# Differential attention: head outputs normalized once per head with tokens on partitions, and the second softmax map scaled by two factors in one GpSimd operation

## The chip, the cores and the metric

The kernel runs on one core of a Trainium2 chip. The time is the device time of one execution in microseconds (us). Five engines matter: TensorE (PE, matmuls), VectorE (DVE), ScalarE (ACT), GpSimd (POOL) and SyncE (SP, which here only issues DMAs). Each engine works through its own instructions in order and waits on semaphores of the others. DMAs of one issuing queue are requested in order.

## The reference, cut to what matters

A trunk of two layers on a sequence of 1024 tokens with model width 1024. The change lies in the first layer's differential attention with 12 heads: each head has two softmax maps, whose difference, weighted by a learned `lam_full`, is applied to the values; the result of every token and head is then normalized over its 128 channels.

```python
def diff_attention(u, positions, lam, subln_g, lambda_init):
    ...
    lam_full = jnp.exp(jnp.sum(lf[0] * lf[1])) - jnp.exp(jnp.sum(lf[2] * lf[3])) + lambda_init
    ...
        p = jax.nn.softmax(s, axis=-1)
        w = p[:, :, 0] - lam_full * p[:, :, 1]
        return jnp.einsum('bhqk,bkhe->bqhe', w.astype(v.dtype), v)
    ...
    o = rms_norm(o, subln_g) * (1.0 - lambda_init)

def rms_norm(x, g):
    xf = x.astype(jnp.float32)
    y = xf * lax.rsqrt(jnp.mean(xf * xf, axis=-1, keepdims=True) + EPS)
    return (y * g.astype(jnp.float32)).astype(x.dtype)
```

Around it stand an input projection, a memory attention, a gate `silu(gate)` and an output projection; the second layer has multi-scale pooling in place of the attention.

## The kernel before

**Stages.** A prologue normalizes the input and builds tables (rotary angles, and `lambda_full`, L571, which leaves the pair `coef` = [1, −lam_full] on every partition). Then the attention stage runs head by head; its end leads into the memory attention, the output projection of layer 0, and layer 1.

**Precision.** Activations and weights are split into a high and a low part (`hh`/`hl`, `wh`/`wl`, `kb`/..., suffix h and l), and each product is made of three passes (`mm3`, L120 to L127). Making a low part is one subtraction on POOL or DVE (L118 for weights: `wl_q`, `wl_k`, `wl_v`, `wl_ga`).

**Order.** PE's instructions stand in the order in which the program is written (`manual_schedule` for PE). For DVE, ACT, POOL and SP a scheduler sets the order. To keep PE busy, the next head's projections (q, k, the gate `ga`, v) are cut into steps, each of three matmuls of 128x512, and `self.step(n)` puts n steps between the attention's own matmuls; there are 64 steps per head. `self.hooks` is a list of small pieces of work with due times counted in steps; `run_hooks`, called once per group of the head's loop, runs one that is due.

**One head.** `attention_layer` goes over the query blocks in pairs p = 3, 2, 1, 0, and over key pairs jj up to p. `score_block` computes the scores of one block of 128 queries (PE L851), masks and exponentiates them (`e`, DVE L856, ACT L865; the sums of the exponentials lie in `st`), and `combine` (L871) makes of the two maps one weight matrix: reciprocal of the two sums (L875), times `coef` (L876), map 1 scaled on POOL (L877), map 0 scaled and added on DVE (L880). `turn_weights` transposes the weights on PE (`wt`, L902) and splits them (`wth` L905, `wtl` L906); `apply_weights` multiplies with the values (L925) into `o`, which holds 128 channels on the partitions and 512 tokens in the row: half a head's tokens.

**Behind each half.** After p = 2 (half 1) and p = 0 (half 0) `attend_post` (L929) squares `o` on ACT (`sq`, L937), multiplies `o` by the learned gain and the gate on DVE (`og`, L938), and splits `sq` into `sqh` (ACT, L939) and `sql` (POOL, L940). It leaves a hook `norm`, due 7 steps later. `norm` multiplies a 128x128 matrix of ones by `sqh` and `sql` (PE, L947), so that every partition holds the sums of all 512 tokens; four DVE instructions (L951) take 32 partitions each and lay four stretches of 128 tokens under one another into `rsx`, 128x128, with the mean and EPS; `newton` (L234 to L241) makes the reciprocal square root in ten DVE steps; four of its rows, one per stretch, are stored to DRAM (`rs`, SP, L956), read back broadcast to all partitions (`z`, SP, L958), multiplied with `og` on POOL (L959) and stored for the output projection (`store_z`, L608).

**Beside it.** The rotary part of the next head: the projected q and k go through ACT to `rotq`/`rotk`, are multiplied by the table on POOL (L767), combined on DVE (`fk`, L764 and L768), and written as the split key `kb` (L802, L803), which the scores read. The reciprocal square root of a few columns is also made elsewhere, by `mean_square` (PE, L250: float32 matmuls with one column per 128 tokens) and `rsqrt_small` (tiles `ms_h`, `rsxh`, `rsyh`, `rsuh`). At the end of the attention stage SP loads the memory tokens (`mf`, L462), DVE splits them (L469, `ml`) and scales the memory query (`mqf`, L620), while PE runs the projections of the remaining gates (`ga`).

Of the kernel before, what the change touches and what calls it, by code (L numbers as in the profile page):

```python
# [10 lines left out]
F32 = mybir.dt.float32  # L11
F32R = mybir.dt.float32r
# [3 lines left out]
ALU = mybir.AluOpType  # L16
# [4 lines left out]
P = 128  # L21
# [3 lines left out]
HALF = 512  # L25
NH = 12
MH = 4
MEM = 256
EPS = 1e-6
# [19 lines left out]
class Trunk:  # L49
# [11 lines left out]
    def build(self):  # L61
# [6 lines left out]
        self.turns = []  # L68
        self.hh = [[None] * KT, [None] * KT]
# [218 lines left out]
    def setup(self):  # L288
        nc, tc, a, const = self.nc, self.tc, self.a, self.const
# [33 lines left out]
        self.rs_dram = [  # L323
            [self.dram.tile([4, P], F32, name=f"rs_{h}_{half}") for half in range(2)]
            for h in range(NH)
        ]
# [10 lines left out]
    def prologue(self, pool):  # L337
# [13 lines left out]
        def hidden(half, ks):  # L351
            for d in ks:
# [3 lines left out]
                    (("sq", 1), ("og", 2), ("es", 4)), alone=half == 1, by=None if half else (None, nc.vector)[d % 2],  # L356
# [214 lines left out]
    def lambda_full(self, sp):  # L571
        nc, a = self.nc, self.a
        lam = sp.tile([P, HALF], F32, tag="z", name="lam")[:, :256].rearrange(
# [3 lines left out]
        prod = sp.tile([P, HALF], F32, tag="sq", name="lam_prod")[:, :128].rearrange(  # L577
# [293 lines left out]
    def combine(self, i, es, st):  # L871
# [4 lines left out]
        nc.vector.tensor_tensor(st[:, 3, :], st[:, 3, :], self.coef, op=ALU.mult)  # L876
        nc.gpsimd.tensor_scalar(  # L877
            es[1][:, :n], es[1][:, :n], st[:, 3, 1:2], 1.0, op0=ALU.mult, op1=ALU.mult
# [50 lines left out]
    def attend_post(self, pool, h, half, o, g):  # L929
        nc = self.nc  # L930
        nm = f"{h}{half}"
        sq = pool.tile([P, HALF], F32, tag="sq", name=f"sq{nm}")
        sh = pool.tile([P, HALF], F32R, tag="sqh", name=f"sqh{nm}")
        sl = pool.tile([P, HALF], F32R, tag="sql", name=f"sql{nm}")
        og = pool.tile([P, HALF], F32, tag="og", bufs=2, name=f"og{nm}")
# [3 lines left out]
        nc.scalar.copy(sh, sq)  # L939
        nc.gpsimd.tensor_tensor(sl, sq, sh.bitcast(F32), op=ALU.subtract)  # L940

        def norm():


            t = self.tb(f"ms{nm}")
            for i, part in enumerate((sh, sl)):
                nc.tensor.matmul(t, self.ones_r, part, start=(i == 0), stop=(i == 1))  # L947
            x = pool.tile([P, P], F32, tag="rsxa", name=f"rsx{nm}")
            for j in range(4):
                p = slice(32 * j, 32 * j + 32)  # L950
                nc.vector.tensor_scalar(  # L951
                    x[p, :], t[p, j * P : (j + 1) * P], 1.0 / P, EPS, op0=ALU.mult, op1=ALU.add
                )
            y = self.newton(pool, x, P, "a")
            row = self.rs_dram[h][half]
# [752 lines left out]
```

## Time and profile before

| | before |
|---|---|
| median of three runs | 1843.32 us (1841.23 to 1845.65) |
| the profiled execution | 1850.51 us, of which the profile's span is 1848.7 us |
| mean granted clock of TensorE | 0.978 |
| DVE, work of the changed code: L876 | 96 instructions, 36.3 us busy |
| DVE: L951 | 96 instructions, median 286 ns |
| POOL: L877, L940, L959 | 76.6 us (x96), 31.9 us (x24), 31.3 us (x24) |
| ACT: L937, L939 | 14.5 us (x24), 14.9 us (x24) |

The first row is what a change is judged by; the profile is a single execution and gives the durations of single instructions. Busy times of different engines lie beside each other and don't add up to the span. In a list of instructions each row has the start, the length, the engine, the line, the operation, what is written and read (buffer numbers left out), and the shapes; in brackets the idle time of the engine before it and what ended that. A wait reads "engine, tile and line that waited <- who ended the wait: total us, times, longest us".

### The profile page before, as it was taken

Reading aid. Unit: us, or ns where it says so; the run is one execution under the profiler, and the core shown is the slowest. Engines: PE = TensorE matmul, PEld = TensorE weight load, DVE = VectorE, ACT = ScalarE, POOL = GpSimd, SP = SyncE. Lnnn points to the kernel's source line nnn. Section 1 sums busy time; section 2 is a strip of 40 time slices with the busy share of each in tenths; the row PEclk is TensorE's granted clock in tenths of the full one; section 3 lists DMA queues with packets and bytes.
Section 4 is the critical chain, followed back from the end, with each engine's and each line's share of the span. In section 5 each row is a group of like instructions: output and inputs, shape, how many; then the busy total and the mean of one; then the engine's idle time right before and its main releaser. Section 6 shows DMA issues by size and latency. Waiting matters only on the chain.

```text
span 1848.7 us, 24838 instructions
## 1 busy us (share of the span) xinstructions
PE 1744.1 (94%) x8478; PEld 1449.6 (78%) x8478; DVE 1351.3 (73%) x2705; ACT 950.3 (51%) x1764; POOL 660.3 (36%) x563
## 2 busy tenths in 40 slices
PE   6899999999999999999999998997999999979997
PEld 4788888888888888888777886875788777768886
DVE  7778789788888889876657768688876667754513
ACT  6667667657657656743246546453443332224422
POOL 4334444444434344442241243300133433413452
PEclk9999999999999999999999999998999999989998
DMA  5011111111111111112463878643312121156542
GB/s 184 23 35 54 42 44 58 46 46 47 46 46 57 36 52 52 40 64 68 152 202 121 268 255 266 224 143 108 103 61 89 55 88 66 54 173 196 171 150 95
DMA packets 81679, 188.68 MB, mean 102 GB/s; under 512 B 9200, under 2 KB 17104, under 8 KB 81552
## 3 DMA queue, kind: packets, MB, share of 16 engines
q1 hardware_dynamic: 79296, 183.08, 30.2%
q10 hardware_dynamic: 2160, 3.75, 0.6%
q8 instruction: 67, 1.10, 0.2%
q14 instruction: 60, 0.49, 0.1%
q0 software_dynamic: 96, 0.26, 0.0%
HBM read 155.29 MB, written 31.77 MB: 101 GB/s over the span
## 4 chain that ended last, share of the span: by engine, by line
PE 67%; DVE 19%; ACT 6%; DMA 5%; issue 3%; POOL 0%; SPq 0%; DVEq 0%; ACTq 0%; POOLq 0%
PE s L851 4%; PE o L925 3%; PE ob L127 3%; PE ob L125 3%; PE ob L126 3%; PE ga L125 3%; PE ga L126 3%; PE ga L127 3%; DMA zf<-z 2%; PE v L125 2%; PE v L127 2%; PE v L126 2%; PE wt L902 2%; ACT rotq L763 2%; DVE e L856 2%
## 5 line engine op out<-in xcount | busy, mean ns | idle before, releaser
L865 ACT ACTIVATE e<-e,st 128x640 f32<-128x640 f32 (+4 forms) x192 | 148.2, 773 | 111.7 <-DVE st L856 110.7
L118 POOL TENSOR_TENSOR wl_o<-wf_o,wh_o 128x384 fp32r<-128x384 f32 x64 | 98.8, 1544 | 238.4 <-ACT wh_o L115 210.9
L877 POOL TENSOR_SCALAR e<-e,st 128x640 f32<-128x640 f32 (+4 forms) x96 | 76.6, 798 | 199.1 <-DVE st L876 116.0
L1539 DVE TENSOR_TENSOR zr<-zf,zr 128x512 fp32r<-128x512 f32 x132 | 108.9, 843 | 42.8 <-ACT zr L1538 42.6
L118 DVE TENSOR_TENSOR wl_o<-wf_o,wh_o 128x640 fp32r<-128x640 f32 x64 | 59.3, 926 | 104.9 <-ACT wh_o L115 100.5
L1538 ACT CAST zr<-zf 128x512 fp32r<-128x512 f32 x132 | 80.8, 619 | 87.7 <-DMA zf<-z 60.7
L905 ACT CAST wth<-wt 128x512 fp32r<-128x512 f32 (+2 forms) x168 | 72.5, 432 | 103.4 <-PE wt L902 73.8
L115 ACT CAST wh_o<-wf_o 128x1024 fp32r<-128x1024 f32 x64 | 67.2, 1049 | 112.9 <-PE ob L126 68.4
L856 DVE CUSTOM_DVE_ANT_0 e<-s,mask 128x512 f32<-128x512 f32 (+2 forms) x192 | 109.5, 581 | 11.6 <-PE s L851 10.0
L125 PE MATMUL ga<-hh,wh_ga 128*128 128x512 f32 x256 | 105.0, 410 | 3.7 <-DVE mqf L620 3.7
L127 PE MATMUL ob<-zr,wl_o 128*128 128x512 f32 x256 | 101.0, 394 | 6.0 <-DVE wl_o L118 6.0
L127 PE MATMUL ga<-hh,wl_ga 128*128 128x512 f32 x256 | 101.6, 397 | 0.0
L126 PE MATMUL ga<-hl,wh_ga 128*128 128x512 f32 x256 | 101.5, 397 | 0.0
L851 PE MATMUL s<-kb,qa 128*128 128x512 f32 (+2 forms) x288 | 98.6, 349 | 2.9 <-DVE kb L803 2.9
L125 PE MATMUL ob<-zr,wh_o 128*128 128x512 f32 x256 | 100.8, 394 | 0.1
L126 PE MATMUL ob<-zr,wh_o 128*128 128x512 f32 x256 | 100.5, 393 | 0.0
L851 PE MATMUL s<-kb,qlo 128*128 128x512 f32 (+2 forms) x288 | 98.4, 349 | 0.0
L125 PE MATMUL k<-hh,wh_k 128*128 128x512 f32 x192 | 79.5, 414 | 8.3 <-ACT wh_k L115 8.3
L906 DVE TENSOR_TENSOR wtl<-wt,wth 128x512 fp32r<-128x512 f32 (+2 forms) x168 | 82.7, 492 | 5.8 <-ACT wth L905 4.5
L880 DVE SCALAR_TENSOR_TENSOR e<-e,st,e 128x640 f32<-128x640 f32 (+4 forms) x96 | 77.9, 811 | 9.8 <-POOL e L877 9.1
L902 PE MATMUL wt<-cst,e 128*128 128x128 f32 x432 | 69.7, 275 | 14.4 <-DVE e L880 11.9
L125 PE MATMUL q<-hh,wh_q 128*128 128x512 f32 x192 | 79.5, 414 | 0.0
(1226 smaller groups left out, 5657.0 us busy)
## 6 DMA issues: line engine op xcount, KB each, us to landing
zf<-z SPq DMA_DIRECT2D x132, 256.0 KB, 4.4
wf_o<-in_w_out SPq DMA_DIRECT2D x64, 512.0 KB, 3.9
wf_ga<-in_w_in SPq DMA_DIRECT2D x16, 512.0 KB
wf_q<-in_w_in SPq DMA_DIRECT2D x12, 512.0 KB, 3.3
wf_v<-in_w_in SPq DMA_DIRECT2D x12, 512.0 KB, 3.8
z<-rs SPq DMA_DIRECT2D x24, 256.0 KB, 3.2
z<-z SPq DMA_DIRECT2D x24, 256.0 KB, 2.0
wf_k<-in_w_in SPq DMA_DIRECT2D x11, 512.0 KB, 3.1
```

Source lines behind the costliest of these rows:

```text
L118: eng.tensor_tensor(wl[:, c], wf[:, c], wh[:, c].bitcast(F32), op=ALU.subtract)
L125: nc.tensor.matmul(out, sh, mh, start=first, stop=False, skip_group_check=more)
L126: nc.tensor.matmul(out, sh, ml, start=False, stop=False, skip_group_check=more)
L127: nc.tensor.matmul(out, sl, mh, start=False, stop=last, skip_group_check=more)
L851: nc.tensor.matmul(sc[m][:, w], q[half][part][:, m, qs], k[kh][:, m, w], start=(part == 0), stop=(part == 1),)
L856: nc.vector.tensor_tensor_reduce(out=es[m][:, lo:hi], in0=sc[m][:, : hi - lo], in1=self.mask[:, S - n + lo : S - n + hi], scale=1.0, scala ...
L865: nc.scalar.activation(es[m][:, :n], es[m][:, :n], AF.Exp, bias=least[m], scale=-1.0, accum_out=st[:, 2, m : m + 1],)
L880: nc.vector.scalar_tensor_tensor(es[0][:, :n], es[0][:, :n], st[:, 3, 0:1], es[1][:, :n], op0=ALU.mult, op1=ALU.add)
L902: nc.tensor.transpose(t[:, c : c + P], w[b][:, j * P : (j + 1) * P], self.ident)
L906: nc.vector.tensor_tensor(wl[:, lo:hi], t[:, lo:hi], wh[:, lo:hi].bitcast(F32), op=ALU.subtract)
L1538: nc.scalar.copy(z[:, 0, :], zf)
L1539: nc.vector.tensor_tensor(z[:, 1, :], zf, z[:, 0, :].bitcast(F32), op=ALU.subtract)
```

## The change

`attend_post` no longer splits the squares. For half 1 it only keeps `sq` and `og` in a list `self.posts`; behind half 0 it leaves one hook for the whole head. That hook turns the product around: the squares are the stationary side, 128 tokens at a time, and a column `inv_v` of 1/128 is the moving side, so each of 8 float32 matmuls gives the mean squares of 128 tokens, one per partition; the eight fill a tile of 128x8. `rsqrt_small` adds EPS and runs the same ten steps on 128x8. The result is stored with its two dimensions exchanged into an [8, 128] tensor in DRAM, which needs a transfer of 1024 single elements; two broadcast reads, two products and two stores follow. In `combine` the product with `coef` goes: the first map's factor was 1.0 throughout, and the second's is now the second per-partition operand of the POOL instruction, where a constant 1.0 stood. `sq`, `og` and `z` get one buffer more each.

```diff
@@ prologue, accumulate_square(...)
-                    (("sq", 1), ("og", 2), ("es", 4)), ...
+                    (("sq", 2), ("og", 3), ("es", 4)), ...
@@ combine
         nc.vector.reciprocal(st[:, 3, :], st[:, 2, :])
-        nc.vector.tensor_tensor(st[:, 3, :], st[:, 3, :], self.coef, op=ALU.mult)
         nc.gpsimd.tensor_scalar(
-            es[1][:, :n], es[1][:, :n], st[:, 3, 1:2], 1.0, op0=ALU.mult, op1=ALU.mult
+            es[1][:, :n], es[1][:, :n], st[:, 3, 1:2], self.coef[:, 1:2],
+            op0=ALU.mult, op1=ALU.mult,
         )
@@ attend_post
-        nc.scalar.copy(sh, sq)
-        nc.gpsimd.tensor_tensor(sl, sq, sh.bitcast(F32), op=ALU.subtract)
+        self.posts.append((half, sq, og))
+        if half:
+            return
+        posts, self.posts = self.posts, []
 
         def norm():
-            t = self.tb(f"ms{nm}")
-            for i, part in enumerate((sh, sl)):
-                nc.tensor.matmul(t, self.ones_r, part, start=(i == 0), stop=(i == 1))
-            x = pool.tile([P, P], F32, tag="rsxa", name=f"rsx{nm}")
-            for j in range(4):
-                p = slice(32 * j, 32 * j + 32)
-                nc.vector.tensor_scalar(
-                    x[p, :], t[p, j * P : (j + 1) * P], 1.0 / P, EPS, op0=ALU.mult, op1=ALU.add
+            t = self.tb(f"ms{nm}")[:, :8]
+            for half, sq, _ in posts:
+                for j in range(4):
+                    c = 4 * half + j
+                    nc.tensor.matmul(
+                        t[:, c : c + 1], sq[:, j * P : (j + 1) * P], self.inv_v,
+                        start=True, stop=True,
+                    )
+            y = self.rsqrt_small(pool, t, 8, "a")
+            nc.sync.dma_start(self.rs_dram[h].rearrange("c t -> t c"), y)
+            rows = self.rs_dram[h].rearrange("c t -> (c t)")
+            for half, _, og in posts:
+                z = pool.tile([P, HALF], F32, tag="z", bufs=2, name=f"z{h}{half}")
+                nc.sync.dma_start(
+                    z, rows[half * HALF : (half + 1) * HALF].partition_broadcast(P)
                 )
-            y = self.newton(pool, x, P, "a")
-            row = self.rs_dram[h][half]
-            nc.sync.dma_start(row, y.rearrange("(j r) t -> j r t", j=4)[:, 0, :])
-            z = pool.tile([P, HALF], F32, tag="z", name=f"z{nm}")
-            nc.sync.dma_start(z, row.rearrange("j t -> (j t)").partition_broadcast(P))
-            nc.gpsimd.tensor_tensor(z, z, og, op=ALU.mult)
-            self.store_z(0, h, half, z)
+                nc.gpsimd.tensor_tensor(z, z, og, op=ALU.mult)
+                self.store_z(0, h, half, z)
```

Lines of the changed kernel are two lower than before from the rotary part to `apply_weights` (L765 is before's L767, L878 its L880), and one higher from `load_w` to the steps of `newton`. What the change moves is shown at three places around the norm of one head, while the next head's key is projected.

PE, before: the norm of the head's second half (half 0) stands between two steps of the key's projection.

```order
L127 MATMUL k_2999<-hh_284,wl_k_2818 128x512
L947 MATMUL ms_3061<-sqh_2934,ones_r 128x512
L947 MATMUL ms_3061<-sql_2935,ones_r 128x512
L125 MATMUL k_2999<-hh_291,wh_k_2817 128x512
L126 MATMUL k_2999<-hl_292,wh_k_2817 128x512
```

PE, in the changed kernel, the same place; `sq_2596` and `sq_2813` are the squares of the two halves.

```order
L127 MATMUL k_2874<-hl_273,wh_k_2698 128x512
L128 MATMUL k_2874<-hh_272,wl_k_2699 128x512
L947 MATMUL ms_2935<-inv_v,sq_2596 128x1 x4
L947 MATMUL ms_2935<-inv_v,sq_2813 128x1 x4
L126 MATMUL k_2874<-hh_279,wh_k_2698 128x512
L127 MATMUL k_2874<-hl_280,wh_k_2698 128x512
```

Eight matmuls of one column stand where two of 512 columns stood; the pair of the head's other half, some 20 steps earlier, is gone from its place.

DVE, before, from the reciprocal of a block with 768 keys to the product that completes its weights. `rsua` and `rsya` are the steps of the reciprocal square root.

```order
L875 RECIPROCAL st_3024<-st_3024 128x2
L856 ISA e_3129,st_3128<-s_3131,mask 128x512
L856 ISA st_3128 128x1
L241 SCALAR_TENSOR_TENSOR rsya<-rsua,rsya 128x128
L876 TENSOR_TENSOR st_3024<-st_3024,coef 128x2
L856 ISA e_3130,st_3128<-s_3132,mask 128x512
L856 ISA st_3128 128x1
L239 TENSOR_TENSOR rsua<-rsx_3064,rsya 128x128
L764 SCALAR_TENSOR_TENSOR fk_3090<-k_2999,trig_tab 128x512
L240 SCALAR_TENSOR_TENSOR rsua<-rsua,rsya 128x128
L880 SCALAR_TENSOR_TENSOR e_3025<-e_3025,st_3024,e_3026 128x768
```

DVE, in the changed kernel, from shortly ahead of the same reciprocal to the same product (now L878).

```order
L235 TENSOR_SCALAR rsya<-rsxa 128x8
L240 TENSOR_TENSOR rsua<-rsxa,rsya 128x8
L241 SCALAR_TENSOR_TENSOR rsua<-rsua,rsya 128x8
L242 SCALAR_TENSOR_TENSOR rsya<-rsua,rsya 128x8
L240 TENSOR_TENSOR rsua<-rsxa,rsya 128x8
L241 SCALAR_TENSOR_TENSOR rsua<-rsua,rsya 128x8
L873 RECIPROCAL st_2899<-st_2899 128x2
L242 SCALAR_TENSOR_TENSOR rsya<-rsua,rsya 128x8
L240 TENSOR_TENSOR rsua<-rsxa,rsya 128x8
L241 SCALAR_TENSOR_TENSOR rsua<-rsua,rsya 128x8
L242 SCALAR_TENSOR_TENSOR rsya<-rsua,rsya 128x8
L878 SCALAR_TENSOR_TENSOR e_2900<-e_2900,st_2899,e_2901 128x768
```

The masks of the next block (L856) and the first rotary product of the key (L764) stood ahead of the product; now only four of the small steps stand between the reciprocal and it, and the masks follow.

POOL, before, from that block's scaling to the product that makes `z`.

```order
L877 TENSOR_SCALAR e_1598<-e_1598,st_1596 128x768
L767 TENSOR_TENSOR rotk_1661<-rotk_1661,trig_tab 128x512
L877 TENSOR_SCALAR e_1702<-e_1702,st_1700 128x512
L118 TENSOR_TENSOR wl_v_1767<-wf_v_1764,wh_v_1766 128x1024
L767 TENSOR_TENSOR rotk_1750<-rotk_1750,trig_tab 128x512
L959 TENSOR_TENSOR z_1654<-z_1654,og_1508 128x512
```

POOL, in the changed kernel, the same stretch.

```order
L874 TENSOR_SCALAR e_1541<-e_1541,st_1539,coef 128x768
L765 TENSOR_TENSOR rotk_1610<-rotk_1610,trig_tab 128x512
L959 TENSOR_TENSOR z_1599<-z_1599,og_1237 128x512
L959 TENSOR_TENSOR z_1603<-z_1603,og_1454 128x512
L874 TENSOR_SCALAR e_1651<-e_1651,st_1649,coef 128x512
L119 TENSOR_TENSOR wl_v_1715<-wf_v_1712,wh_v_1714 128x1024
L765 TENSOR_TENSOR rotk_1698<-rotk_1698,trig_tab 128x512
```

Both products of the head (L959) moved ahead of the next block's scaling, the low part of the value weights and the second rotary product. On SP the `rs` store is followed by both reads and then by both stores of `z`; before, a half's store of `z` came behind its own read, and a weight load could stand between them.

More of the change, by code (lines that the diff above doesn't have):

```diff
@@ L68, in build @@
         self.turns = []
+        self.posts = []
         self.hh = [[None] * KT, [None] * KT]
@@ L322, in setup @@
         ]
[L323 to L326, printed above, removed]
+        self.rs_dram = [self.dram.tile([8, P], F32, name=f"rs_{h}") for h in range(NH)]
         self.trig_dram = self.dram.tile([4, 32, 2, S // 4], F32, name="trig_all")
@@ L355, in hidden @@
                     pool, xs[half, d], sums[half], d, f"x{half}{d}",
-                    (("sq", 1), ("og", 2), ("es", 4)), alone=half == 1, by=None if half else (None, nc.vector)[d % 2],
+                    (("sq", 2), ("og", 3), ("es", 4)), alone=half == 1, by=None if half else (None, nc.vector)[d % 2],
                     add=nc.vector if d > 3 else None,
@@ L572, in lambda_full @@
         nc, a = self.nc, self.a
-        lam = sp.tile([P, HALF], F32, tag="z", name="lam")[:, :256].rearrange(
+        lam = sp.tile([P, HALF], F32, tag="z", bufs=2, name="lam")[:, :256].rearrange(
             "p (a b) -> p a b", a=4
@@ L576, in lambda_full @@
         nc.gpsimd.dma_start(lam, a["attn_lambda"].rearrange("o (a b) -> o a b", a=4)[0].partition_broadcast(P))
-        prod = sp.tile([P, HALF], F32, tag="sq", name="lam_prod")[:, :128].rearrange(
+        prod = sp.tile([P, HALF], F32, tag="sq", bufs=2, name="lam_prod")[:, :128].rearrange(
             "p (a b) -> p a b", a=2
@@ L931, in attend_post @@
         nm = f"{h}{half}"
[L932 to L935, printed above, removed]
+        sq = pool.tile([P, HALF], F32, tag="sq", bufs=2, name=f"sq{nm}")
+        og = pool.tile([P, HALF], F32, tag="og", bufs=3, name=f"og{nm}")
         with self.tc.high_priority(offset=SOON):
```

## The prediction, made before the changed kernel had run

> **What bounds the kernel now.** The page first, for the busy shares:
>
> ```profile
> span 1848.7 us, 24838 instructions
> PE 1744.1 (94%) x8478; PEld 1449.6 (78%) x8478; DVE 1351.3 (73%) x2705; ACT 950.3 (51%) x1764; POOL 660.3 (36%) x563
> ```
>
> TensorE (PE) has work 94% of the span. That is a mean over stages, so the next view is the table by stretches (time, then busy time and count of PE, weight load, DVE, ACT, POOL; granted clock) for two heads' worth of the attention stage, where the changed code runs:
>
> ```profile
> 230.00:370.00 140.00, 138.16 (x729) 117.02 (x728) 119.94 (x298) 92.41 (x182) 59.12 (x60) 1.00 0.15 50
> ```
>
> Here PE stands idle for 1.84 us of 140 at full clock. So this stage is as long as PE's own work plus PE's waits; what other engines save counts only where PE waits for them. The list of PE's waits, asked for the attention stage (90 to 870), for its end (840 to 960) and for the beginning, names three that the change can reach:
>
> ```profile
> PE wt L902 <- DVE e L880: 11.9, 11, 2.0
> PE ga L125 <- DVE mqf L620: 3.7, 1, 3.7
> PE bc_h L530 <- DVE rsyh L241: 6.2, 1, 6.2
> ```
>
> The first comes once per head, eleven times; the second once, at the end of the stage; the third before the heads begin. The change is therefore summed in five terms: PE's work, the wait on `e`, a new risk on GpSimd (POOL), the end, the beginning.
>
> **Term 1: PE's work, +10.8 us.** Twice per head two matmuls with 512 columns go. PE's timeline, rows as start, length:
>
> ```profile
> 298.90 0.40 PE L947 MATMUL ms<-sqh,ones_r 128*128 128x512 f32 x1
> ...
> 299.37 0.39 PE L125 MATMUL k<-hh,wh_k 128*128 128x512 f32 x1
> ```
>
> The pair occupies 299.37 − 298.90 = 0.47 us, so 0.94 per head goes. In come 8 matmuls with one column, in float32. Before has the same form elsewhere, at L250:
>
> ```profile
> 20.97 1.95 PE L250 MATMUL ms_h<-inv_d,ssqx 128*128 128x1 f32 x16
> 22.78 0.48 PE L125 MATMUL q<-hh,wh_q 128*128 128x512 f32 x1
> 23.09 0.39 PE L126 MATMUL q<-hl,wh_q 128*128 128x512 f32 x1
> ```
>
> Sixteen records there are 8 instructions of the program (a float32 matmul leaves two). They hold PE for 22.78 − 20.97 = 1.81 us, and the next matmul comes 0.31 later instead of 0.23, so 1.81 to 1.89. Net per head: +0.9; times 12 heads, **+10.8** (10.4 to 11.4). Nothing hides it, since PE is the bound. One column in float32 takes 1.81 / 8 = 0.226 us, as much as 512 columns did (half of 0.47): the product is small, but it is no cheaper for PE.
>
> **Term 2: the wait on `e`, −10.4 us.** DVE's timeline around one of the eleven, PE's row that waited, PE's wait of this kind up to 110 us, and all of L951 from the view of its tile:
>
> ```profile
> 303.29 0.23 DVE L234 TENSOR_SCALAR rsya<-rsx 128x128 int32<-128x128 int32 x1
> 304.08 0.16 DVE L875 RECIPROCAL st<-st 128x2 f32<-128x2 f32 x1
> 306.98 0.78 DVE L240 SCALAR_TENSOR_TENSOR rsua<-rsua,rsya 128x128 f32<-128x128 f32 x1
> 307.69 1.00 DVE L880 SCALAR_TENSOR_TENSOR e<-e,st,e 128x768 f32<-128x768 f32 x1
> 308.75 0.55 PE L902 MATMUL wt<-cst,e 128*128 128x128 f32 x3 [0.90 <-DVE e L880]
> PE wt L902 <- DVE e L880: 2.0, 1, 2.0
> L951 DVE TENSOR_SCALAR rsx<-ms x96: 269/286/298, 142.5 to 878.9; 32x128 f32<-32x128 f32 x96
> ```
>
> L880 started at 307.69 because the reciprocal square root on 128x128 stood ahead of it: four L951 at 0.286, then ten steps, one of them stretched to 0.78. Also gone is the product L876 between reciprocal and POOL's L877. In the changed order the ten steps work on 128x8:
>
> ```profile
> 1836.32 0.16 DVE L239 TENSOR_TENSOR rsuh<-rsxh,rsyh 128x4 f32<-128x4 f32 x1
> 1836.51 0.16 DVE L240 SCALAR_TENSOR_TENSOR rsuh<-rsuh,rsyh 128x4 f32<-128x4 f32 x1
> 305.41 0.91 POOL L877 TENSOR_SCALAR e<-e,st 128x768 f32<-128x768 f32 x1 [3.45 <-DVE st L876]
> ```
>
> A small step takes 0.2 from start to start. `e` no longer waits for long ones: the reciprocal comes at about 304.1, POOL's product ends near 305.3, and L880 with its 1.00 near 306.3. PE wanted it 0.90 before 308.75, at 307.85, and the little matmuls shift that by 1.4: 2.9 us to spare. Ten of the waits should go whole; the first (2.0 us, before any norm has run) loses only some 0.5, by L876. So 11.9 − 1.5 = **10.4** (0 if DVE's queue still holds `e` back, 11.9 at most). The other norm of the head, in the middle, hid no PE wait: nothing is late next there.
>
> **Term 3: POOL's queue, +2.2 us.** By the printed order the two `z` products now stand directly behind the first `rotk`, ahead of `e`, `wl_v` and the second `rotk`, whose rotated key PE's scores need. POOL takes its instructions in order, so all these wait for the broadcast `z`. The rows of the chain (SP's queue, POOL, DVE, PE):
>
> ```profile
> 311.40 0.50 SPq L956 DMA_DIRECT2D rs<-rsya  x1
> 313.02 0.32 SPq L958 DMA_DIRECT2D z<-rs  x1
> z<-rs SPq DMA_DIRECT2D x24, 256.0 KB, 3.2
> L959 POOL TENSOR_TENSOR z<-z,og 128x512 f32<-128x512 f32 x24 | 31.3, 1303 | 33.9 <-DMA z<-rs 28.7 <-issue 5.2
> 310.53 0.70 POOL L877 TENSOR_SCALAR e<-e,st 128x512 f32<-128x512 f32 x1 [2.92 <-ACT kb L802]
> 312.29 2.83 POOL L118 TENSOR_TENSOR wl_v<-wf_v,wh_v 128x1024 fp32r<-128x1024 f32 x1 [1.06 <-ACT wh_v L115]
> 315.08 1.75 POOL L767 TENSOR_TENSOR rotk<-rotk,trig_tab 128x512 f32<-128x512 f32 x1
> 320.24 0.69 DVE L803 TENSOR_TENSOR kb<-fk,kb 64x512 fp32r<-64x512 f32 x1
> 321.49 0.39 PE L851 MATMUL s<-kb,qa 128*128 128x512 f32 x1
> ```
>
> Step by step: L951's 1.1 ahead of 303.29 is gone, so the steps begin at 302.2; eleven at 0.2, with POOL's 0.91 in their way, give the result at 305.4. From the store of `rs` to the request of `z` 1.6, plus X; landing 3.2; two products 2.6; `e` 0.7; `wl_v` 2.6; `rotk` 1.3 to 1.75: it ends at 317.5 + X against 316.8 before. The key `kb` is then there at about 320.9 + X, and PE asks for it near 321.8 (321.49 + 1.4 from the matmuls − 1.1 from the wait). PE waits max(0, X − 0.9), and each of my steps is good to ±0.7 in sum.
>
> X is what storing `rs` takes longer. Before stores 4 rows of 512 bytes; the change stores 1024 separate 4-byte words. No transfer of that kind is in this trace. The nearest is the old store itself, alone in a stretch of 3 us (350 to 353):
>
> ```profile
> DMA packets 8, 0.00 MB, mean 1 GB/s; under 512 B 4, under 2 KB 8, under 8 KB 8
> q1 hardware_dynamic: 8, 0.00, 0.3%
> q1 hardware_dynamic: 79296, 183.08, 30.2%
> ```
>
> 0.3% of 16 engines in 3 us is 0.144 us for 8 packets, 18 ns each. With 64 words per engine that is X = 1.1. The far end is the mean packet of the whole run, 0.302 × 1848.7 × 16 / 79296 = 113 ns, or 7.2 us, though those packets carry 2.3 KB; below, X could be −0.2 if issue takes 0.32 instead of 0.50. I take 1.1, the row of the same store: 0.2 us of waiting, eleven times, **+2.2** (0 to +69; at twice 18 ns, +15).
>
> The Trainium skill speaks against this edit: "DMA: Bandwidth & Descriptors", in "Rules for kernel authors", says that a strided last dimension becomes one descriptor per element and should be rearranged to be contiguous. Its section "Bandwidth" puts a floor of about 10.5 ns on a packet; 64 of them would be an estimated 0.7 us, and the sum below would be 2 us lower. No transfer in the trace of before decides between that and 18 ns.
>
> **Term 4: the end of the stage, −4.2 us.** Behind the last head's norm nothing of the next head covers the chain:
>
> ```profile
> 880.88 2.37 DVE L240 SCALAR_TENSOR_TENSOR rsua<-rsua,rsya 128x128 f32<-128x128 f32 x1
> 885.57 0.50 SPq L956 DMA_DIRECT2D rs<-rsya  x1
> 892.56 1.00 SPq L462 DMA_DIRECT2D mf<-in_mem  x2
> 903.40:909.00 5.60, 5.58 (x14) 4.45 (x15) 4.59 (x6) 0.00 (x0) 0.00 (x0) 0.55 0.33 129
> ```
>
> SP asks for `mf` only behind the `z` stores, and DVE reaches `mqf` (L620) behind `mf`'s work: PE's 3.7 us. With short steps the store of `rs` goes out near 882.5, though two products follow it; `mf` is requested at 890.7 + X, 1.9 − X earlier, and PE arrives 1.4 later. The wait becomes 0.4 + X = 1.5: −2.2. After the long wait the last row shows the clock at 0.55 for 5.6 us, worth up to 0.45 × 5.6 = 2.5; a 1.5 us wait should not cost it, and I take −2.0. Bounds 0 and −6.2. (The Trainium skill, "TensorE: Matmul & The Clock Gate", "Part 1: The HAM clock gate", puts the drop at an idle window of about 3.4 us. By that rule the 3.7 us wait halves the clock, the trace's 0.55 agrees, and 1.5 us would not.)
>
> **Term 5: the beginning, +0.9 us.** The scheduler now places the four operations on lambda, first and last here, in front of the third wait's chain:
>
> ```profile
> 43.86 0.29 DVE L580 TENSOR_TENSOR lam_prod<-lam 128x128 f32<-128x128 f32 x1
> 44.93 0.15 DVE L586 TENSOR_SCALAR coef<-coef 128x1 f32<-128x1 f32 x1
> 37.81 2.30 DVE L241 SCALAR_TENSOR_TENSOR rsyh<-rsuh,rsyh 128x4 f32<-128x4 f32 x1
> ```
>
> Two at 0.29 and two at 0.15 are 0.9 ahead of `rsyh`, for which PE waits. A short step can be stretched to 2.30, so −1 to +3.
>
> Nothing else counts. The 24 casts (ACT) and 24 subtractions (POOL) that go lie beside PE's work; the shares (51% and 36%) say that neither is short of room. POOL's L877 with a second factor per partition has no row: 0.70 for 512 columns as now, or as slow as the two-tensor product, 1.30. I take 0.70.
>
> **Sum.** +10.8 − 10.4 + 2.2 − 4.2 + 0.9 = −0.7. The profiled execution took 1850.5 us (span 1848.7) and would take 1849.8; the median shown is 1843.3, 0.4% less, and the difference carries over: **1842.6**. Against no change 0.2% (3.7 us) is about what a measurement can tell, so this is "the same".
>
> **Rivals.** (a) Slower: POOL's queue becomes the bound, by the store of 1024 words. It decides from X = 0.9 and shows from X = 1.5. At 36 ns a word, X = 2.3: 11 × 1.4 = 15.4 instead of 2.2, and 1.2 more at the end: 1857. For it: the `z` products really stand ahead of `rotk`, and a packet's cost is an average over eight. Against: 18 ns is of this very queue. Chance 0.24. (b) L877 at 1.30: the chain ahead of `rotk` grows by 0.6, 11 × 0.6 + 0.6 = +7.2, 1849.8; its 768 columns take 1 us longer, and the wait on `e` keeps 1.9 us to spare. 0.05. (c) The change does not shorten the wait on `e`: 1842.6 + 10.4 = 1853. Against it stands the order, in which only short steps are left ahead of L880. 0.04. (d) Faster: X under 0.9 (−2.2), the end's full gain (−2.0 more), lambda hidden (−0.9), matmuls at the low bound (−0.4): 1837.1. 0.25. The forecast keeps 0.42.
>
> The range 1835.5 to 1860 takes in (a) to X = 2.5, (b), (c), and (d) with a little below; X beyond that (0.06) and a larger gain at the end (0.05) stay outside. Faster 0.25, same 0.42, slower 0.33.
>
> **What would show it.** Term 1: eight records' pairs of 128x1 over 1.8 us once per head. Term 2: no row `PE wt <- DVE e` but the first head's. Term 3: time from `rs` to `z` in SP's queue, 1.6 + X, and PE's wait `s <- kb`, which is nothing now inside the heads. Term 4: PE's wait for `mqf` near 1.5 and no clock of 0.55 behind it. Term 5: PE's wait for `rsyh` near 7. A time from `rs` to `z` above 4 us would make the forecast wrong at once; so would PE records of 128x1 much shorter than 0.11 each.

## The result, and the profile after

| | before | after |
|---|---|---|
| median | 1843.84 us (4 runs, 1841.23 to 1845.65) | 1968.14 us (4 runs, 1965.47 to 1971.48) |
| ratio to before, 95% interval | | 1.0664, 1.0644 to 1.0685 |
| profiled execution, span | 1850.51, 1848.7 us | 1965.47, 1963.7 us |
| mean granted clock of TensorE | 0.978 | 0.954 |

The change costs 124 us where 1 us of gain was forecast, far outside the range. The page of after, its span, engines, and the DMA queue (packets, MB, share of 16 engines):

```profile
span 1963.7 us, 24750 instructions
PE 1777.5 (91%) x8622; PEld 1479.2 (75%) x8622; DVE 1237.3 (63%) x2405; ACT 939.7 (48%) x1742; POOL 628.5 (32%) x539
...
q1 hardware_dynamic: 91584, 183.08, 28.1%
z<-rs SPq DMA_DIRECT2D x24, 256.0 KB, 3.5
```

DVE, ACT and POOL all have less to do, as intended, and PE's share fell. The queue moved the same 183.08 MB in 12,288 packets more: 1024 for each of 12 heads. The stretches that answer to those of before (time; busy time and count of PE, weight load, DVE, ACT, POOL; clock) show where it went:

```profile
230.00:370.00 140.00, 123.12 (x633) 104.35 (x632) 87.41 (x212) 77.22 (x152) 46.88 (x47) 0.93 0.13 42
336.70:345.60 8.90, 0.33 (x2) 0.00 (x0) 3.41 (x2) 0.00 (x0) 6.72 (x5) 0.74 0.36 119
345.60:351.00 5.40, 5.33 (x16) 4.47 (x17) 4.16 (x13) 2.74 (x7) 1.39 (x4) 0.50 0.24 90
```

PE's 138.16 us of work in 140 became 123.12. The second row is a hole: 8.9 us with two matmuls. The third is what follows it, matmuls at half clock. PE's waits in the attention stage, then at its end:

```profile
PE ga L126 <- DVE fk L762: 83.5, 10, 8.7
PE wt L900 <- DVE e L878: 2.1, 1, 2.1
...
PE ga L126 <- DVE mqf L618: 9.3, 1, 9.3
```

The wait on `e` is gone but for the first head, as forecast, and a wait seven times as large has come. It can be followed backwards through the engines in one head. SP's queue, POOL, DVE and PE, as start, length:

```profile
324.70 0.38 SPq L952 DMA_DIRECT2D rs<-rsya  x1
335.53 1.62 SPq L956 DMA_DIRECT2D z<-rs  x2
```

```profile
338.78 2.62 POOL L959 TENSOR_TENSOR z<-z,og 128x512 f32<-128x512 f32 x2 [11.81 <-DMA z<-rs]
341.39 0.77 POOL L874 TENSOR_SCALAR e<-e,st,coef 128x512 f32<-128x512 f32 x1
342.12 2.34 POOL L119 TENSOR_TENSOR wl_v<-wf_v,wh_v 128x1024 fp32r<-128x1024 f32 x1
```

```profile
342.19 2.82 DVE L878 SCALAR_TENSOR_TENSOR e<-e,st,e 128x512 f32<-128x512 f32 x1 [11.02 <-POOL e L874]
344.93 0.68 DVE L762 SCALAR_TENSOR_TENSOR fk<-k,trig_tab 128x512 f32<-128x512 f32 x1
```

```profile
345.67 0.80 PE L126 MATMUL ga<-hh,wh_ga 128*128 128x512 f32 x1 [8.63 <-DVE fk L762]
346.26 0.63 PE L127 MATMUL ga<-hl,wh_ga 128*128 128x512 f32 x1
346.69 0.63 PE L128 MATMUL ga<-hh,wl_ga 128*128 128x512 f32 x1
```

From the store of `rs` to the request of `z` there are 10.83 us instead of 1.62. POOL stands 11.81 us before its two `z` products; the scaling of `e` behind them comes late, DVE stands behind that, and `fk` (L762), which empties the PSUM bank of the projected key, comes late too; PE needs that bank for `ga`. Behind the hole the matmuls are 0.43 apart instead of 0.23.

The length of a head is the distance of its `rs` stores: here nine heads of before and nine of after.

```profile
177.10 0.52 SPq L956 DMA_DIRECT2D rs<-rsya  x1
...
781.75 0.50 SPq L956 DMA_DIRECT2D rs<-rsya  x1
```

```profile
169.88 0.38 SPq L952 DMA_DIRECT2D rs<-rsya  x1
...
868.37 0.38 SPq L952 DMA_DIRECT2D rs<-rsya  x1
```

(781.75 − 177.10) / 9 = 67.18 and (868.37 − 169.88) / 9 = 77.61: **10.4 us per head**. Of that, 8.35 is the wait (83.5 / 10), +0.9 the narrow matmuls, −1.0 the wait on `e` that went (8.8 us in the nine heads of before), and 2.2 are left. The slow clock accounts for about that much: 5.4 us at 0.50 in the head shown are worth 2.7, and not every head has as long a stretch.

### The profile page after: what moved, and what is told of

It is laid out like the page before. It is cut to its first block, busy times and chain, and to the rows that moved or that the text cites. A ratio compares the mean times of both kernels' runs of the same rounds, so it can differ in the third digit from the quotient of the medians.

```text
span 1963.7 us, 24750 instructions
## 1 busy us (share of the span) xinstructions
PE 1777.5 (91%) x8622; PEld 1479.2 (75%) x8622; DVE 1237.3 (63%) x2405; ACT 939.7 (48%) x1742; POOL 628.5 (32%) x539
## 3 DMA queue, kind: packets, MB, share of 16 engines
q1 hardware_dynamic: 91584, 183.08, 28.1%
## 4 chain that ended last, share of the span: by engine, by line
PE 34%; DVE 9%; DMA 5%; issue 1%; ACT 1%; POOL 0%; SPq 0%; DVEq 0%; ACTq 0%; POOLq 0%
PE ob L128 3%; PE ob L126 3%; PE ob L127 3%; DMA zf<-z 2%; PE oc L126 1%; PE oc L127 1%; PE oc L128 1%; PE oa L126 1%; PE oa L127 1%; PE oa L128 1%; DVE ws L1403 1%; PE grp L126 1%; PE grp L128 1%; PE grp L127 1%; PE ga L126 1%
## 5 line engine op out<-in xcount | busy, mean ns | idle before, releaser
L126 PE MATMUL ga<-hh,wh_ga 128*128 128x512 f32 x256 | 113.9, 445 | 92.8 <-DVE fk L762 83.5
L878 DVE SCALAR_TENSOR_TENSOR e<-e,st,e 128x640 f32<-128x640 f32 (+4 forms) x96 | 101.1, 1054 | 134.5 <-POOL e L874 134.4
L874 POOL TENSOR_SCALAR e<-e,st,coef 128x640 f32<-128x640 f32 (+4 forms) x96 | 84.4, 879 | 151.9 <-DVE st L873 147.0
L126 PEld LDWEIGHTS ga<-hh,wh_ga 128*128 128x128 f32 x256 | 53.7, 210 | 105.1 <-DVE fk L762 87.8
L127 PE MATMUL ga<-hl,wh_ga 128*128 128x512 f32 x256 | 107.9, 422 | 0.0
L128 PE MATMUL ga<-hh,wl_ga 128*128 128x512 f32 x256 | 107.4, 419 | 0.0
L800 ACT CAST kb<-fk 64x512 fp32r<-64x512 f32 x48 | 29.6, 617 | 122.6 <-DVE fk L766 122.0
```

Source lines behind the costliest of these rows:

```text
L126: nc.tensor.matmul(out, sh, mh, start=first, stop=False, skip_group_check=more)
L127: nc.tensor.matmul(out, sh, ml, start=False, stop=False, skip_group_check=more)
L128: nc.tensor.matmul(out, sl, mh, start=False, stop=last, skip_group_check=more)
L874: nc.gpsimd.tensor_scalar(es[1][:, :n], es[1][:, :n], st[:, 3, 1:2], self.coef[:, 1:2], op0=ALU.mult, op1=ALU.mult,)
L878: nc.vector.scalar_tensor_tensor(es[0][:, :n], es[0][:, :n], st[:, 3, 0:1], es[1][:, :n], op0=ALU.mult, op1=ALU.add)
```

## The experiments

**Is it the store, and what of it?** Five runs keep the changed kernel's instructions and their order from the first head on, and alter only how the 1024 (or 512) results are laid into DRAM. None of the five gives every token its own factor. The code leaves out the declaration of `rs_dram` and, where it only follows the layout, the line with `rows`.

e1_runs32: each partition's eight values as one run.

```diff
-            nc.sync.dma_start(self.rs_dram[h].rearrange("c t -> t c"), y)
+            nc.sync.dma_start(self.rs_dram[h], y)          # rs_dram[h]: [P, 8]
...
```

> The changed kernel, but the 128x8 result is stored as it lies: 128 runs of 32 bytes instead of 1024 of 4. The reads stay contiguous, so every token gets the factor of another one; the instructions and their order are those of the changed kernel. Theory A (each run costs a DMA engine a fixed time; 10.83 - 1.62 = 9.2 us over 64 runs per engine is 144 ns each): 8 runs per engine, so from the store's issue to the read's issue about 1.6 + 1.0 = 2.7 us, PE's wait ga <- fk under 0.5 us per head instead of 8.4, and a time of 1843 to 1852. Theory B (the time comes from the order on POOL or from the narrow matmuls, the store is incidental): still above 1930.

e2_runs8: pairs of values as a run.

```diff
-            nc.sync.dma_start(self.rs_dram[h].rearrange("c t -> t c"), y)
+            nc.sync.dma_start(self.rs_dram[h].rearrange("c t w -> t c w"),   # rs_dram[h]: [4, P, 2]
+                              y.rearrange("t (c w) -> t c w", w=2))
...
```

> The changed kernel with 512 runs of 8 bytes for the same 1024 words (the order of tokens is changed as a consequence). Theory A (price per run): store to read 1.6 + 4.6 = 6.2 us, PE's wait ga <- fk about 4.0 us per head, a time of 1895 to 1920, the lower end if the clock no longer drops behind the wait. Theory C (price per word or byte, not per run): store to read stays near 10.8 us and the time near 1968.

e5_half4: half the words.

```diff
-            nc.sync.dma_start(self.rs_dram[h].rearrange("c t -> t c"), y)
+            nc.sync.dma_start(self.rs_dram[h][0:4, :].rearrange("c t -> t c"), y[:, 0:4])
...
-                    z, rows[half * HALF : (half + 1) * HALF].partition_broadcast(P)
+                    z, rows[0:HALF].partition_broadcast(P)
```

> The changed kernel storing only four of the eight columns: 512 runs of 4 bytes, 32 per DMA engine; both reads take those 512 words, so half 1 of each head gets the factors of half 0. Theory A1 (the number of runs sets the price; 32 per engine with 8 bytes took 4.2 us from store to read): about 4.2 us again and a time near 1881. Theory F (a 4-byte run has a price of its own, 9.2 us over 64 runs or 144 ns): 1.5 + 4.6 = 6.1 us and a time of 1895 to 1910.

e6_ownline: each partition's words in 64 bytes of its own.

```diff
-            nc.sync.dma_start(self.rs_dram[h].rearrange("c t -> t c"), y)
+            nc.sync.dma_start(self.rs_dram[h][:, 0:16:2], y)     # rs_dram[h]: [P, 16]
...
```

> The changed kernel storing all 1024 words in runs of 4 bytes, but each partition's eight words into its own 64 bytes of DRAM, every other word (the rest was filled with zeros in the prologue by 12 small DMAs; the reads take the first 1024 words of that area, so the factors are not the right ones). Theories A1 and F (only the number and size of the runs count): 10.5 to 11.3 us from store to read and a time of 1960 to 1975. Theory G (words of different partitions that lie in the same 64 bytes hinder each other): under 7 us and a time under 1910.

e11_spread: each word in 64 bytes of its own.

```diff
-            nc.sync.dma_start(self.rs_dram[h].rearrange("c t -> t c"), y)
+            nc.sync.dma_start(self.rs_dram[h][:, 0:P:16], y)     # rs_dram[h]: [P, P]
...
```

> The changed kernel storing 1024 runs of 4 bytes, every word into 64 bytes of its own (the area was filled from a weight matrix in the prologue; the reads take its first 1024 words, so the factors are not the right ones). Theory G2 (from the five stores so far: about 0.06 us for each run of an engine and about 0.4 us for each word that shares 64 bytes): about 4 us from store to read and a time of 1870 to 1890. Theory F2 (a run of 4 bytes costs what it costs, sharing does not matter): 6.4 us or more, as with e6_ownline, and a time of 1925 or more.

What they gave, with before, after and e8 (told below) beside them. "Store to read" is from the issue of `rs` to that of `z` in the head near 310 us, "behind the packets" the part of it that lies behind the last packet of the store (median of the heads), "landing" the median of the reads, "sum" store to read and landing, all in us; the head is measured as above.

| | runs, bytes | words or runs in the same 64 bytes | store to read | behind the packets | landing | sum | head | median, ratio to before |
|---|---|---|---|---|---|---|---|---|
| before | 4 of 512 | | 1.62 | 0.39 | 3.2 | 4.8 | 67.18 | |
| e1_runs32 | 128 of 32 | 2 | 1.45 | 0.40 | 3.4 | 4.9 | 67.11 | 1843.97, 0.9985 (0.9973 to 0.9996) |
| e8_runs16 | 256 of 16 | 4 | 1.66 | 0.49 | 3.9 | 5.6 | 70.56 | 1889.74, 1.0224 |
| e11_spread | 1024 of 4 | 1 | 3.78 | 1.69 | 3.4 | 7.2 | 68.50 | 1884.3, 1.0203 |
| e2_runs8 | 512 of 8 | 8 | 4.20 | 2.85 | 3.7 | 7.9 | 69.95 | 1881.42, 1.0194 |
| e6_ownline | 1024 of 4 | 8, of one partition | 6.33 | 4.41 | 3.5 | 9.8 | 73.39 | 1935.73, 1.0484 |
| e5_half4 | 512 of 4 | 16 | 8.80 | 7.46 | 5.5 | 14.3 | 78.01 | 1974.3, 1.0693 |
| after | 1024 of 4 | 16 | 10.83 | 8.89 | 3.5 | 14.3 | 77.61 | 1968.14, 1.0664 |

The medians of e6 and e11 hold some 15 to 20 us of the prologue that fills the area (their first `rs` store comes at 185.80 and 190.24, that of after at 169.88), so the column of the head is the one to compare. The two ends of the table, SP's rows of e1 and of e11:

```profile
304.49 0.33 SPq L952 DMA_DIRECT2D rs<-rsya  x1
305.94 0.80 SPq L956 DMA_DIRECT2D z<-rs  x2
```

```profile
327.12 0.53 SPq L954 DMA_DIRECT2D rs<-rsya  x1
330.90 0.81 SPq L958 DMA_DIRECT2D z<-rs  x2
```

Where in the store does the time lie? The DMA packets of after in the head shown, asked for 325.6 to 326.3 us and for 326.3 to 335.5, which is the request of the read (packets and their sizes, then the queue and the share of 16 engines):

```profile
DMA packets 1040, 0.00 MB, mean 6 GB/s; under 512 B 1040, under 2 KB 1040, under 8 KB 1040
q1 hardware_dynamic: 1040, 0.00, 66.9%
```

```profile
DMA packets 1, 0.01 MB, mean 1 GB/s; under 512 B 0, under 2 KB 0, under 8 KB 0
q14 instruction: 1, 0.01, 0.5%
```

All packets of the store, 1024 words and 16 more, 65 per engine, start within 0.68 us, one each 10.5 ns; then the queue `q1` moves nothing for 9.2 us until SP requests the read (the one packet in that time is of another queue). **The engines are quick with the single words; what became long is the time behind the last packet, until the store counts as done:** 0.39 us in before, 8.89 in after.

e1 settles where the 124 us come from: with the store in runs of 32 bytes and nothing else touched, the loss is gone. Theory B falls. Theory A was right about e1's time, but it expected 2.7 and 6.2 us from store to read for e1 and e2, which took 1.45 and 4.20. Half the runs with 8 bytes (e2) are far cheaper; half the runs with 4 bytes (e5) are not cheaper at all: the read is requested 2 us sooner, but its first packet comes 3.1 us behind the request instead of 1.0, and the head is as long as with 1024 words. (Two of the twelve heads of after show the same exchange: the read is requested after 8.5 us and its first packet comes 2.7 to 2.9 us behind that.) A price per run cannot do that; both expectations for e5 missed. What e5 shares with the change is that the words lie side by side, 16 in each 64 bytes. e6 and e11 keep the number and size of the runs and spread the words over more of DRAM, 8 and 64 KB instead of 4: with 8 words in 64 bytes the sum falls from 14.3 to 9.8, with one word to 7.2. **Of the 9.5 us that the change adds to the chain from store to landed read, 7.1 go when the words are spread out, and 2.4 stay with 1024 separate runs** (7.2 − 4.8).

So theory G holds in that neighbouring words hinder each other, but not as it was put: e6, where 64 bytes belong to one partition alone, came to 6.33 us as forecast, yet without the filling of its area still to about 1920 us instead of under 1910, and its sum is 2.6 us above e11's. Words of one partition hinder each other too. The size of 64 bytes is this document's way of counting; counted within 32, 128 or 512 bytes the stores come in the same order, and no run tells words that share a block from words that merely lie close. Why neighbours hinder each other, the records don't show. The Trainium skill, "DMA: Bandwidth & Descriptors", "Specifications", says that an engine reads, modifies and writes below 512 bytes; words that wait for one another's turn on the same place would fit that, and no run here shows the turns themselves.

**Does the slow store hurt by itself, or only through POOL's queue?** e3_late leaves it as slow and moves the products (the code is shortened).

```diff
-                nc.gpsimd.tensor_tensor(z, z, og, op=ALU.mult)
-                self.store_z(0, h, half, z)
+                zs.append((half, z, og))
+        self.hooks.append((self.count + 26, finish))
+    def finish():       # run behind a score block of the next head, st its sums
+        nc.vector.tensor_scalar(one, st[:, 3, 0:1], 0.0, 1.0, op0=ALU.mult, op1=ALU.add)
+        for half, z, og in zs:
+            nc.gpsimd.tensor_scalar(og, og, one, self.coef[:, 0:1], op0=ALU.mult, op1=ALU.mult)
+            nc.gpsimd.tensor_tensor(z, z, og, op=ALU.mult)
+            self.store_z(0, h, half, z)
```

> The changed kernel, output as the reference: the slow store stays, but the two z products of a head (and an extra multiplication of og by 1.0, with a factor that depends on a score block of the next head) stand some 24 us later in POOL's order, behind the next head's rotk, wl_v and wl_q. Theory A (the slow store hurts only because POOL's queue stands behind it, and the clock falls behind PE's wait): store to read still 10.8 us, PE's wait ga <- fk gone, time 1840 to 1850. Theory D (the slow store also holds up SP's queue with the weight loads, or the DMA engines): above 1880, with PE waiting for weights.

POOL's rows of one head and the wait at the end of the stage:

```profile
307.63 0.77 POOL L875 TENSOR_SCALAR e<-e,st,coef 128x512 f32<-128x512 f32 x1 [1.56 <-DVE st L874]
...
332.42 1.29 POOL L974 TENSOR_TENSOR z<-z,og 128x512 f32<-128x512 f32 x1
```

```profile
PE ga L127 <- DVE mqf L619: 10.4, 1, 10.4
```

Median 1853.59, ratio 1.0034 (1.0020 to 1.0048). Store to read is 11.3 us there, yet a head takes 66.78 us, less than before: the scaling of `e` (first row) goes ahead at once, the products follow 25 us later without waiting, and the wait `ga <- fk` is gone. Theory D falls. The miss against 1840 to 1850 is the end of the stage, where no next head hides the chain: 10.4 us of waiting instead of 3.7, with a slow clock behind it. So the store's slowness is a cost of latency, and the scheduler's place for the products made it a cost of PE.

**Which edit removed the wait on `e`?** e4_combine takes only the second edit into the kernel before; e7_oldcombine takes it out of e1.

```diff
         nc.vector.reciprocal(st[:, 3, :], st[:, 2, :])
-        nc.vector.tensor_tensor(st[:, 3, :], st[:, 3, :], self.coef, op=ALU.mult)
         nc.gpsimd.tensor_scalar(
-            es[1][:, :n], es[1][:, :n], st[:, 3, 1:2], 1.0, op0=ALU.mult, op1=ALU.mult
+            es[1][:, :n], es[1][:, :n], st[:, 3, 1:2], self.coef[:, 1:2], op0=ALU.mult, op1=ALU.mult
         )
```

> The kernel before with the change in combine alone (L876 gone, POOL's scaling with two factors per partition); norm as before. Theory A: POOL's instruction keeps its length within 0.1 us, so the product e comes 0.2 to 0.5 us sooner in ten heads; PE's wait wt <- e falls from 11.9 to 7 to 10 us, time 1838 to 1842. Rival E (two factors per partition slow POOL to the rate of a two-tensor product, 0.6 us more for 512 columns): the wait on e grows and the time is 1846 to 1852.

The same edit undone in e1 is e7:

```diff
         nc.vector.reciprocal(st[:, 3, :], st[:, 2, :])
+        nc.vector.tensor_tensor(st[:, 3, :], st[:, 3, :], self.coef, op=ALU.mult)
...
-            es[1][:, :n], es[1][:, :n], st[:, 3, 1:2], self.coef[:, 1:2], op0=ALU.mult, op1=ALU.mult
+            es[1][:, :n], es[1][:, :n], st[:, 3, 1:2], 1.0, op0=ALU.mult, op1=ALU.mult
```

> The run with 32-byte runs (e1), with combine as before the change (L876 back, POOL's scaling with one factor): norm's short steps alone. The reason given in the prediction (the long steps ahead of the product e made PE wait): the wait wt <- e stays gone but for the first head, at most 2.5 us in all, and the time is that of e1 within 0.2%. Rival (L876 alone held e back): the wait returns to 0.4 to 0.9 us in ten heads and the time is 4 to 9 us above e1.

PE's waits on `e` in the attention stage, of e4 and of e7:

```profile
PE wt L902 <- DVE e L880: 1.4, 1, 1.4
PE ga L125 <- DVE fk L764: 0.6, 2, 0.3
```

```profile
PE wt L900 <- DVE e L878: 2.0, 1, 2.0
```

e4: 1844.37, ratio 0.9983 (0.9969 to 0.9997). e7: 1848.46, ratio 1.0012 (1.0000 to 1.0024). Either edit alone removes the wait in all heads but the first; neither theory of e4 foresaw that it would go entirely. But the 10 us of waiting did not become 10 us of time: e4's head is 66.99 us, 0.2 shorter, and its gain is about 3 us. PE's busy time per head rose from 66.22 to some 66.7. Added up over nine heads, PE's rows stand 1.2 us per head closer together at `wt`, but 0.4 further apart at `ga`, 0.3 at `o` and 0.3 where `ga` follows `k`: small gaps that the records count as work, and a few short waits such as `ga <- fk`. Why PE is held up there instead is not shown. e7 lies 5 us above e1, as the rival for e7 said, though its wait stayed away, as the theory said, and its 0.2% for the time did not hold: there too the list of waits does not tell the time.

**What do the narrow matmuls cost?** In e8_runs16 a partition gets four neighbouring tokens, which allows 16-byte runs in the right order.

```diff
-                        t[:, c : c + 1], sq[:, j * P : (j + 1) * P], self.inv_v,
+                        t[:, c : c + 1], sq[:, j::4], self.inv_v,
...
-            nc.sync.dma_start(self.rs_dram[h].rearrange("c t -> t c"), y)
+            nc.sync.dma_start(self.rs_dram[h].rearrange("s t j -> t s j"),    # rs_dram[h]: [2, P, 4]
+                              y.rearrange("t (s j) -> t s j", s=2))
```

> Output as the reference. Each of the 8 matmuls takes every fourth token of its half as stationary columns, so one partition holds four neighbouring tokens and the store has 256 runs of 16 bytes, 16 per engine. Theory A1: between 1.45 us (8 runs per engine) and 4.2 us (32): 1.8 to 2.5 us from store to read, no PE wait inside the heads, 1841 to 1847. Rival (loading weights with a step of 16 bytes is slower): the 16 records take clearly more than 1.7 us and each 1 us more adds 12 to the time.

The store was quick (1.66 us from store to read in the head of the table, 1.57 to 3.10 over the twelve heads), but the rival won, and more than won. PE's timeline and the stretches around it:

```profile
304.51 3.66 PE L947 MATMUL ms<-inv_v,sq 128*128 128x1 f32 x16
308.03 0.77 PE L126 MATMUL k<-hh,wh_k 128*128 128x512 f32 x1
308.61 0.63 PE L127 MATMUL k<-hl,wh_k 128*128 128x512 f32 x1
309.03 0.63 PE L128 MATMUL k<-hh,wl_k 128*128 128x512 f32 x1
```

```profile
304.00:308.00 4.00, 4.00 (x19) 3.91 (x18) 3.10 (x8) 3.35 (x6) 0.00 (x0) 0.92 0.02 6
308.00:312.00 4.00, 4.00 (x13) 3.42 (x14) 1.87 (x12) 3.28 (x8) 0.08 (x1) 0.50 0.05 5
```

The 16 records take 3.52 us instead of 1.70, and behind them the clock is at 0.50, although PE had waited for nothing. A head is 3.4 us longer than in e1 with both together.

e9_permuted has ACT lay the squares out instead (the store is that of e8):

```diff
-            nc.scalar.activation(sq, o, AF.Square)
+            nc.scalar.activation(sq.rearrange("p (j t) -> p j t", j=4),
+                                 o.rearrange("p (t j) -> p j t", j=4), AF.Square)
...
-                        t[:, c : c + 1], sq[:, j::4], self.inv_v,
+                        t[:, c : c + 1], sq[:, j * P : (j + 1) * P], self.inv_v,
```

> Output as the reference. As the run with 16-byte runs (e8), but the squares are laid out by ACT (L933 reads o with a step of four tokens), so that the matmuls' stationary columns lie side by side again. If the step in the stationary side was all that cost e8 its time: the 16 records take 1.7 us, the clock stays at 1.00 behind them, store to read 1.6 us, a time equal to e1 (ratio to before 0.996 to 1.000). Rival (ACT reads PSUM with a step more slowly, and o is freed later): L933 well above 0.60 us and a PE wait on o of the same size twice per head, 1850 or more.

1850.55, ratio 1.0019 (1.0006 to 1.0032). The matmuls are at 1.70 us again, the clock stays up, and ACT's instruction still takes 0.60, so neither rival's price shows. It misses e1's time by 6 us all the same. It has nine short waits `ga <- fk`, 4.2 us together, and its reads land in 3.8 us instead of e1's 3.4. PE's rows at `ga` stand 0.6 us per head further apart than in e1, while the head is 0.4 longer (67.53), so the loss lies there; whether the later reads are its cause stays open.

e10_onepass rounds the squares and halves the passes:

```diff
-        sq = pool.tile([P, HALF], F32, tag="sq", bufs=2, name=f"sq{nm}")
+        sq = pool.tile([P, HALF], F32R, tag="sq", bufs=2, name=f"sq{nm}")
...
-                        t[:, c : c + 1], sq[:, j * P : (j + 1) * P], self.inv_v,
+                        t[:, 2 * c : 2 * c + 2], sq[:, j * P : (j + 1) * P], self.inv_vr,   # [P, 2], fp32r
...
-            y = self.rsqrt_small(pool, t, 8, "a")
+            y = self.rsqrt_small(pool, t[:, 0:16:2], 8, "a")
```

> As e9_permuted, but the squares are rounded to the format of the other matmuls (fp32r) and multiplied in one pass with a moving side of two equal columns, so 8 records instead of 16; the output differs from the reference only by that rounding. Term 1 of the prediction (0.11 us per record is PE's price of the narrow matmuls): 8 records take 0.9 us instead of 1.8, 12 heads give back about 11 us: a ratio to before of 0.991 to 0.994. Rival (the price is per instruction, not per record): no change against e9_permuted.

```profile
297.28 0.95 PE L951 MATMUL ms<-inv_vr,sq 128*128 128x2 f32 x8
298.09 0.47 PE L126 MATMUL k<-hh,wh_k 128*128 128x512 f32 x1
...
170.42 0.38 SPq L956 DMA_DIRECT2D rs<-rsya  x1
...
765.58 0.38 SPq L956 DMA_DIRECT2D rs<-rsya  x1
```

**1836.81 us, ratio 0.9949 (0.9930 to 0.9968): 0.5% below the kernel before, and the interval leaves out 1.** Eight records take 298.09 − 297.28 = 0.81 us instead of 1.70, so the price is per record. A head takes (765.58 − 170.42) / 9 = 66.13, 1.0 below e1. Against e9 it gained 1.4 per head, more than the 0.9 of the records; the list of waits has no `ga <- fk` any more, and on POOL the scaling of `e` now stands between the two `z` products. The ratio just missed the forecast of 0.991 to 0.994.

e12_before_onepass asks whether the missing pass alone does it:

```diff
-        nc.scalar.copy(sh, sq)
-        nc.gpsimd.tensor_tensor(sl, sq, sh.bitcast(F32), op=ALU.subtract)
...
-            for i, part in enumerate((sh, sl)):
-                nc.tensor.matmul(t, self.ones_r, part, start=(i == 0), stop=(i == 1))
+            nc.tensor.matmul(t, self.ones_r, sq, start=True, stop=True)     # sq: fp32r; combine as in e4
```

> The kernel before with the change in combine and with the squares rounded to fp32r and summed by one matmul with ones per half instead of two (no sqh, no sql); norm per half, 128x128 steps and row stores as before. If what makes e10_onepass faster is mostly the missing second pass and the product with coef, this has a ratio to before near that of e10: 0.47 us less PE per head on top of e4_combine, 5.6 us, 0.994 to 0.997. If the layout with tokens on partitions brings something of its own: 0.997 or more.

1844.52, ratio 0.9989 (0.9974 to 1.0003). No: almost nothing is gained, and a new wait stands in the list.

```profile
PE s L851 <- DVE st L856: 6.0, 11, 0.8
PE wt L902 <- DVE e L880: 1.5, 1, 1.5
```

PE now waits eleven times for the masks (`st`, L856), for which the long steps that are still on DVE are the likely cause, though no run takes them out of this kernel. Against e10's 0.9949 the two intervals don't meet: the layout with tokens on partitions is worth something once its store is cheap.

## Why the prediction was wrong

**Term 3 failed, in what X is made of.** The mechanism was named: the `z` products ahead of the rest of POOL's queue, waiting for a store of 1024 words, with the point of decision at X = 0.9. X was taken at 1.1 us, "the row of the same store", from 8 packets at 18 ns; it is 10.83 − 1.62 = **9.2**. Even the far end, 7.2 from the 113 ns of the mean packet, was too low. The step that failed is to make X of the packets' time in the DMA engines alone. That time was even sized too high, 1.1 us against 0.68. What lies behind the last packet was kept as it had been, without a reason, and it went from 0.40 us to 9.23 in the head shown. The runs put in its place a store whose completion is late when its words lie side by side (7.1 of the 9.5 us up to the landed read) and when it has many runs (2.4), which no row of before could show. The chance of 0.06 left beyond X = 2.5 was much too small for a transfer of which the trace had no example. The Trainium skill's rule quoted there (one descriptor per element, rearrange) was right, and the trace agrees with 12 × 1024 packets. The Trainium skill's floor of 10.5 ns, quoted there too, agrees with the trace, 0.68 us for 65 packets per engine; it prices the packets, not the wait behind them.

Three smaller parts of the same term. PE did not wait for `kb`, the sign that was named, but for the PSUM bank that `fk` empties. That is another branch behind POOL: it runs through `e` and DVE's order, not through `rotk`, so that the wait of 8.35 comes close to X − 0.9 is in part luck. In the working, `rotk` ends 0.7 us later than before (317.5 against 316.8) and the time of `kb` leaves these 0.7 out, so the point of decision should have been 0.2; and a store of 0.7 us would have lowered the sum by 2.6, not 2. Last, rival (a) left out the clock: a wait of 8.6 us was followed by 5.4 us at 0.50, some 2.2 us per head on average, 24 in all.

**Term 1 held.** 320.31 − 318.61 = 1.70 us in after, and the next matmul 0.32 later instead of 0.23, so 0.85 per head against 0.9:

```profile
318.61 1.84 PE L947 MATMUL ms<-inv_v,sq 128*128 128x1 f32 x16
320.31 0.47 PE L126 MATMUL k<-hh,wh_k 128*128 128x512 f32 x1
320.63 0.39 PE L127 MATMUL k<-hl,wh_k 128*128 128x512 f32 x1
```

The rival that narrow matmuls lower the clock was left out; 1.7 us of them don't, 3.5 us of them did (e8).

**Term 2 held as a wait** (11.9 to 2.1), but e4 and e7 show that either edit alone would have done it, so the wait needed both, the long steps, which the prediction put first, and the product L876. **As time it was too large where it stood alone:** e4 got 3 us of the 10.

**Term 4 turned round.** Its sum needs a quick store. With the slow one the wait grew to 9.3 us; in e1, with X = −0.2, it is gone, as 0.4 + X said.

**Term 5** had the wrong sign, within its range: +0.9 was forecast, and the first `o` matmul comes 0.4 sooner, at 91.02 us instead of 91.43. The wait for `rsyh`, forecast near 7, went, and the wait `s <- kb` has 7.3 instead of 2.9.

**Rival (b)** is answered by the rows quoted: POOL's scaling takes 0.77 us for 512 columns with two factors against 0.70 with one, and not 1.30.

With the right X the sum would have come out: worked out for e1's X it gives −4.2 us (the −0.7 less 2.2 and 1.3), and e1 measured −0.15% (−0.27 to −0.04), −2.8 us. That is agreement of the sum; terms 2 and 5 show that the single terms were not all right.

## What to carry to other kernels

A small transfer is priced by its pattern, not by its bytes: look at the length of its contiguous runs and at how closely short runs lie beside each other, and choose which token a partition holds so that runs stay at 16 bytes or more (1.6 to 3.3 us from store to read in e8 to e10). Ask for the time until a transfer counts as done, not only for its packets. When a step of the sum rests on an operation of which the trace has no example, measure it by itself before the rest, or leave a wide range. Ask for each long latency what an in-order queue has behind it: the same store cost 10 us per head or nothing, depending on where two products stood.

## What the runs showed of the hardware that was not expected

A store of single words is moved quickly and done late: 1040 packets in 0.68 us, and then 8.89 us (median) until the dependent read could be requested. Neighbours count: 512 words took as long as 1024 (14.3 us to the landed read) when 16 lay in each 64 bytes, and 1024 took 7.2 when each lay 64 bytes from the next. A part of the store's cost can appear in the read behind it (landing 5.5 us in e5, 3.5 in after).

The clock fell without a wait: 3.52 us of one-column matmuls with a step of four in the stationary side were followed by a clock of 0.50 (e8). The Trainium skill, "TensorE: Matmul & The Clock Gate", "Part 1: The HAM clock gate", has the clock follow how busy the array has been over windows of about 3.4 us. PE's rows are busy for 4.00 of 4.00 us there, so the run agrees only if loading weights with one column behind them counts as little, which no run shows by itself. The step of 16 bytes itself doubled the time of a float32 record, from 0.11 to 0.22 us.
